# The causal mask ahead of the gates' exponentials: added by VectorE on the way out of PSUM, in place of an identity product on TensorE

## The chip, the cores and the metric

The kernel runs on one core of one Trainium2 chip. The metric is the device time of one execution in microseconds (us). Three runs of the kernel before gave 985.32, 985.60 and 986.42 us, a median of 985.6 us.

## The reference, cut to what matters

The reference is a two-layer encoder trunk on 256 positions of 1024 numbers. Each layer has three sub-layers: a SwiGLU block, a mixer and another SwiGLU block. The mixer has two head groups side by side, a differential attention and an mLSTM. The change is in the mLSTM, in the matrix of weights that a position `j` gives to an earlier position `s`:

```
causal = jnp.tril(jnp.ones((CHUNK, CHUNK), dtype=bool))
D = jnp.where(causal, b[..., :, None] - b[..., None, :] + log_i[..., None, :], -jnp.inf)
m_inter = b + m_prev[..., None]
m = jnp.maximum(m_inter, D.max(-1))
w = jnp.exp(D - m[..., None]) * jnp.einsum('bhcjd,bhcsd->bhcjs', q, k)
```

`exp(D - m)` is wanted, with zero where `s` is later than `j`. The kernel computes the exponent as a product of gate rows, adds a mask that is 0 where `s <= j` and -1e30 elsewhere, and takes the exponential. It works in chunks of 128 positions, of which there are two.

## The kernel before, in words

**Tiling.** The 256 positions are two tiles, `t` = 0 and 1, of 128 rows. A weight arrives in pieces of 128x2048 fp32 numbers, by a DMA that SyncE (SP) issues (L272). Each half of a piece is split in two: ScalarE (ACT) rounds it to a high part `wh` (L278), and VectorE (DVE) subtracts that from the raw half to get the low part `wl` (L279). The activations are split in the same way into `th` and `tl`. Every large product is then three matmuls of 512 columns, high by high, high by low and low by high (`mm3`, L393 to L395), so TensorE (PE) runs thousands of them, and DVE and ACT feed it with split weights.

**The mixer.** `traverse` (L699) walks through 84 steps of three matmuls each. They make six groups of 512 columns: the mLSTM's q and k (ahead of the walk and in its first steps), the attention's q, its k, the mLSTM's v, the attention's v, and the output gate. A group's two tiles end in two PSUM banks, named `pin`, which are read out as soon as they are complete. For the attention's q and k that reading is `rope` (L979): ACT scales the bank into `rv` (L984), DVE multiplies it by the cosines into `ra` (L985) and, in two halves, by the sines into `rb` (L988), and adds the two (L989). `roped` (L992) then transposes the finished `ra` on PE in four blocks (L805), and ACT copies them out as `qkT` (L996).

**What stands between the steps.** The table `AT` gives the step at which each of 32 side stages is written: the gates, the convolution, the rotary transposes, the scores. Both calls of `gate_exps` and the first call of `roped` stand at step 24. `conv` for the q blocks stands at 31, `gate_decays` at 36, `conv_silu` at 38, and `weighted_qk` and the `roped` call for the first tile of k both at 40.

**Order on an engine.** Each engine executes its instructions in the order of its own list. That list is made when the kernel is built: a scheduler takes the program as written, its priorities (`high_priority` around the reading of banks) and its own estimates of durations, and puts the instructions in order. An instruction waits until the ones that it depends on are done, and everything behind it on the same engine waits too.

**The code that the change touches.** `constants_mix` (L178) loads the mask by DMA into a temporary `mraw` (L200), and ACT copies the mask and the 128x128 identity into fp32r tiles, `c_mask` (L203) and `c_identr` (L204). `gate_exps` (L919) runs for each of the two tiles and in each of the two layers, four times in all. It starts a PSUM bank `pe` with a product of the gate rows `ul` and `md` (L924), adds the mask to the bank with a product of the identity and the mask, repeated for the four heads (L925), and ACT takes the exponential of the bank into `eE` (L927, recorded under L256, the line of the helper `func`). `eE` is read in `intra_weights` (L976).

**The stages around it.** `gate_decays` (L930) makes the decays `ex` on DVE (L935 to L937), ACT takes their exponential, and `eh` is their low part (L942). `conv` (L828) is a causal convolution of four blocks, on ACT for its first tap (L834) and on DVE for the other three (L837). `weighted_qk` (L944) starts with two small PE products of `eh` (L949), three small transposes (L952) and two transposes of k (L958). In PE's list these are followed by the four transposes of the `ra` of k's first tile (L805).

Of the kernel before, what the change touches and what calls it, by code (L numbers as in the profile page):

```python
# [15 lines left out]
F32 = mybir.dt.float32  # L16
F32R = mybir.dt.float32r
AF = mybir.ActivationFunctionType
ALU = mybir.AluOpType
# [3 lines left out]
P = 128  # L23
# [28 lines left out]
def _lam_init(l):  # L52
    return 0.8 - 0.6 * math.exp(-0.3 * l)
# [74 lines left out]
class _Trunk:  # L128
# [49 lines left out]
    def constants_mix(self):  # L178
        nc, a = self.nc, self.a
        c1 = self.const.tile([P, sum(math.prod(v) for _, v in C1)], F32, name="c_1")  # L180
        self.after(nc.sync.dma_start(c1, a["c1"]), [self.load])
        at = 0
        for name, shape in C1:
            n = math.prod(shape)
            dims = " ".join("abc"[:len(shape)])
            v = c1[:, at:at + n].rearrange(f"p ({dims}) -> p {dims}", **dict(zip("abc", shape)))
            setattr(self, name, v)
            at += n
        self.scan = self.const.tile([100, 2, S], F32, name="c_scan")
        self.after(nc.sync.dma_start(self.scan.rearrange("p a b -> p (a b)"), a["scan"]), [self.load])  # L190
        for l in range(L):
            nc.gpsimd.tensor_scalar(self.gda[:, l:l + 1], self.gda[:, l:l + 1], 1.0 - _lam_init(l), None, op0=ALU.mult)
        nc.gpsimd.tensor_scalar(self.gml, self.gml, 0.5, None, op0=ALU.mult)
        self.wgc = self.const.tile([P, L, KT, 16], F32R, name="c_wgc")
        ia = nc.scalar.activation(self.wgc[:, :, :, 0:8], self.wg, AF.Copy)
        iv = nc.vector.tensor_tensor(self.wgc[:, :, :, 8:16], self.wg, self.wgc[:, :, :, 0:8].bitcast(F32), op=ALU.subtract)
        self.fold = self.const.tile([16, 8], F32, name="c_fold")
        self.after(nc.vector.tensor_tensor(self.fold, self.ident[0:16, 0:8], self.ident[0:16, 8:16], op=ALU.add), [iv])
        mraw = self.t2("mraw", (P, P))
        self.after(nc.sync.dma_start(mraw, a["mask"]), [self.load])  # L200
        self.mask = self.const.tile([P, P], F32R, name="c_mask")
        self.identr = self.const.tile([P, P], F32R, name="c_identr")
        nc.scalar.activation(self.mask, mraw, AF.Copy)  # L203
        self.after(nc.scalar.activation(self.identr, self.ident, AF.Copy), [ia])  # L204

        lamv = self.t2("lamv", (P, L, 4, 64))
        self.after(nc.sync.dma_start(lamv.rearrange("p l a b -> p l (a b)"), a["lam"].partition_broadcast(P)), [self.load])
        prod = self.t2("lamp", (P, L, 2, 64))
        nc.vector.tensor_tensor(prod, lamv[:, :, 0::2, :], lamv[:, :, 1::2, :], op=ALU.mult)
        sums = self.const.tile([P, L, 2], F32, name="c_lams")  # L210
        nc.vector.tensor_reduce(sums, prod, axis=AX.X, op=ALU.add)
        self.lamsum = sums
        self.neglam = self.const.tile([P, L], F32, name="c_neglam")

        self.g2 = self.ded.tile([P, NT, 2, 4, 32], F32, name="g2")
        nc.gpsimd.memset(self.g2, 0.0)
        self.hot = self.const.tile([100, 4], F32, name="c_hot")
        ih = nc.vector.tensor_reduce(self.hot, self.ident[0:100].rearrange("p (a b) -> p b a", a=4)[:, 0:4, :], axis=AX.X,
                                     op=ALU.add)
        self.after(ih, [iv])  # L220
        self.ul = self.ded.tile([100, S], F32R, name="ul")
        nc.gpsimd.memset(self.ul.bitcast(F32), 0.0)
        for p in (64, 96):
            nc.gpsimd.memset(self.ul[p:p + 4].bitcast(F32), 1.0)
        self.md = self.ded.tile([100, NT, 4, P], F32R, name="md")
        nc.gpsimd.memset(self.md.bitcast(F32), 0.0)
        for t in range(NT):
            i = nc.scalar.activation(self.md[0:36, t], self.hot[0:36].unsqueeze(2).broadcast_to([36, 4, P]), AF.Copy)
            self.after(i, [ia])
        self.hotp = self.const.tile([36, 2, P], F32R, name="c_hotp")  # L230
        self.after(nc.vector.tensor_copy(self.hotp.rearrange("p a (b d) -> p (a b) d", b=2),
                                         self.hot[0:36].unsqueeze(2).broadcast_to([36, 4, 64])), [iv])
        self.qk = self.ded.tile([P, 4, S], F32, name="qk")
        self.qd = self.ded.tile([P, 2, CH], F32, name="qd")
        self.vx = self.ded.tile([P, NT, 4, P + 1], F32, name="vx")
        self.wt = self.ded.tile([P, NT, 2, 2, P], F32, name="wt")
        nc.gpsimd.memset(self.vx, 1.0)
        self.xpad = self.ded.tile([P, 4, S + 3], F32, name="xpad")
        nc.gpsimd.memset(self.xpad[:, :, 0:3], 0.0)
# [444 lines left out]
class _Mixer:  # L684
# [234 lines left out]
    def gate_exps(self, t):  # L919

        tr = self.tr
        cols = slice(t * P, t * P + P)
        pe = tr.bank_bk()
        self.mm(pe, tr.ul[:, cols], tr.md[:, t].rearrange("p h j -> p (h j)"), start=True, stop=False)  # L924
        self.mm(pe, tr.identr, tr.mask.unsqueeze(1).broadcast_to([P, 4, P]), start=False, stop=True)  # L925
        eE = tr.t2("eE")
        tr.func(eE, pe, AF.Exp)  # L927
        self.eE.append(eE)

    def gate_decays(self):  # L930
# [251 lines left out]
```

## Time and profile before

| | kernel before |
|---|---|
| median of three runs | 985.6 us |
| the profiled execution's own time | 986.18 us |
| its span | 984.4 us |
| PE busy | 976.0 us (99%) in 4629 matmuls |
| DVE busy | 606.4 us (62%) in 863 instructions |
| ACT busy | 528.4 us (54%) in 869 instructions |
| GpSimd (POOL) busy | 27.6 us (3%) |
| HBM read | 177.01 MB |
| mean granted PE clock | 0.998 of full speed |

The span runs from the first recorded instruction of the program to its last. The execution's own time is 1.78 us longer, for what lies around the span. "Busy" counts the time in which an engine has an instruction in flight. Matmuls overlap one another, so PE's busy time is not a count of its work: when one matmul takes over from another, the next one's start tells more than its duration. In a list of instructions in order of time, the columns are start and duration in us, engine, line, operation, the tile written and the tiles read, the shape, and how many instructions are merged in the row. What stands in brackets is the engine's idle time ahead of it and what ended it.

### The profile page before, as it was taken

What the parts mean: (1) busy time and instruction counts of PE and PEld (TensorE: products, weight loads), DVE (VectorE), ACT (ScalarE), POOL (GpSimd) and SP (SyncE); (2) the same over time, 40 slices, a digit from 0 to 9 for tenths busy, and PEclk for the clock granted to TensorE, in tenths of its full rate; (3) what the DMA queues carried; (4) which work ended last, traced back from release to release, by engine and by line L of the source; (5) the groups of instructions that cost most, each with busy time, mean ns of one, the idle gap of its engine ahead of it and who ended that gap; (6) DMA issues with size and microseconds to landing.
All of it is one profiled execution on the core that took longest, in us unless ns stands there. A gap on an engine that the chain in (4) does not pass through costs nothing.

```text
span 984.4 us, 12032 instructions
## 1 busy us (share of the span) xinstructions
PE 976.0 (99%) x4629; PEld 800.2 (81%) x4629; DVE 606.4 (62%) x863; ACT 528.4 (54%) x869; POOL 27.6 (3%) x51
## 2 busy tenths in 40 slices
PE   9999999999999999999999999999999999999997
PEld 6888888888788888888888888888888888888885
DVE  6755554589867655555485645455888586554542
ACT  7744444477856545444375544444778475544431
POOL 1000000000010000000000000000001000000000
PEclk9999999999999999999999999999999999999999
DMA  8954545336352844464356455443454257544511
GB/s 304 346 217 174 197 169 192 124 129 216 123 196 95 312 167 179 184 239 171 129 207 242 162 188 207 178 163 119 166 207 167 90 205 263 195 171 171 210 48 43
DMA packets 27640, 178.84 MB, mean 182 GB/s; under 512 B 3034, under 2 KB 4186, under 8 KB 6846
## 3 DMA queue, kind: packets, MB, share of 16 engines
q1 hardware_dynamic: 27006, 177.46, 48.9%
q8 instruction: 36, 0.59, 0.2%
q10 hardware_dynamic: 576, 0.61, 0.2%
q14 instruction: 22, 0.18, 0.0%
HBM read 177.01 MB, written 1.05 MB: 181 GB/s over the span
## 4 chain that ended last, share of the span: by engine, by line
PE 99%; DMA 1%; DVE 0%; SPq 0%; ACT 0%; POOLq 0%; issue 0%; DVEq 0%; ACTq 0%
PE pin L393 21%; PE pin L395 20%; PE pin L394 20%; PE bk L393 10%; PE bk L395 10%; PE bk L394 10%; PE ptr L523 2%; PE ptr L805 1%; PE ptr L412 1%; PE bk L1017 1%; PE bk L1057 1%; DMA x<-in_x_dram 1%; PE bk L372 0%; PE bk L370 0%; PE bk L1097 0%; PE bk L371 0%
## 5 line engine op out<-in xcount | busy, mean ns | idle before, releaser
L279 DVE TENSOR_TENSOR wl<-wr,wh 128x1024 fp32r<-128x1024 f32 x324 | 389.4, 1223 | 223.4 <-ACT wh L278 213.7
L278 ACT ACTIVATE wh<-wr 128x1024 fp32r<-128x1024 f32 x324 | 336.5, 1057 | 190.4 <-PE pin L395 102.1
L393 PE MATMUL pin<-wh,th 128*128 128x512 f32 x880 | 349.5, 398 | 0.0
L395 PE MATMUL pin<-wh,tl 128*128 128x512 f32 x880 | 343.4, 391 | 0.0
L394 PE MATMUL pin<-wl,th 128*128 128x512 f32 x880 | 343.3, 390 | 0.0
L395 PEld LDWEIGHTS pin<-wh,tl 128*128 128x128 f32 x880 | 165.2, 188 | 35.2
L393 PEld LDWEIGHTS pin<-wh,th 128*128 128x128 f32 x880 | 165.4, 188 | 33.3 <-ACT vd L1002 0.8
L394 PEld LDWEIGHTS pin<-wl,th 128*128 128x128 f32 x880 | 165.5, 188 | 32.3
L393 PE MATMUL bk<-wh,hh 128*128 128x512 f32 x352 | 140.0, 398 | 0.0
L395 PE MATMUL bk<-wh,hl 128*128 128x512 f32 x352 | 137.6, 393 | 0.0
L394 PE MATMUL bk<-wl,hh 128*128 128x512 f32 x352 | 137.6, 391 | 0.0
L526 ACT ACTIVATE hh<-ptr 128x256 fp32r<-128x256 f32 x88 | 33.2, 377 | 93.3 <-PE ptr L523 75.6
L256 ACT ACTIVATE sil<-pin,rs 128x256 f32<-128x256 f32 x86 | 40.5, 472 | 73.7 <-PE pin L395 69.8
L395 PEld LDWEIGHTS bk<-wh,hl 128*128 128x128 f32 x352 | 66.1, 188 | 13.8
L394 PEld LDWEIGHTS bk<-wl,hh 128*128 128x128 f32 x352 | 66.2, 188 | 12.8
L393 PEld LDWEIGHTS bk<-wh,hh 128*128 128x128 f32 x352 | 66.1, 188 | 12.8
L527 DVE TENSOR_TENSOR hl<-ptr,hh 128x256 fp32r<-128x256 f32 x88 | 37.1, 422 | 54.3 <-ACT hh L526 51.5
L516 DVE SCALAR_TENSOR_TENSOR h<-pin,rs,sil 128x256 f32<-128x256 f32 x86 | 41.2, 480 | 30.2 <-ACT sil L256 30.2
L401 POOL TENSOR_TENSOR rs<-s,c_half 128x1 f32<-128x1 f32 x24 | 13.1, 553 | 774.2 <-DVE s L438 774.2
L523 PEld LDWEIGHTS ptr<-c,h 128*128 128x128 f32 x176 | 24.7, 140 | 11.5
L523 PE MATMUL ptr<-c,h 128*128 128x128 f32 x176 | 33.4, 271 | 0.0
L454 ACT ACTIVATE junk<-bk 128x512 bf16<-128x512 f32 x24 | 14.2, 592 | 31.1 <-PE bk L395 31.1
(179 smaller groups left out, 586.8 us busy)
## 6 DMA issues: line engine op xcount, KB each, us to landing
wr<-in_w_dram SPq DMA_DIRECT2D x162, 1024.0 KB, 4.9
gpost<-in_gpost_dram SPq DMA_DIRECT2D x6, 512.0 KB, 6.2
wr<-in_w_dram SPq DMA_DIRECT2D x2, 512.0 KB, 7.1
wr<-in_w_dram SPq DMA_DIRECT2D x3, 256.0 KB, 5.2
x<-in_x_dram SPq DMA_DIRECT2D x3, 256.0 KB, 5.8
out_dram<-x SPq DMA_DIRECT2D x2, 256.0 KB, 2.1
x<-in_x_dram SPq DMA_DIRECT2D x2, 128.0 KB, 2.7
wr<-in_w_dram ACTq DMA_DIRECT2D x1, 256.0 KB, 3.5
```

The costliest lines, as they stand in the source:

```text
L256: i = self.nc.scalar.activation(*args, **kw)
L278: ia = nc.scalar.activation(hi, raw[:, j], AF.Copy)
L279: iv = nc.vector.tensor_tensor(lo, raw[:, j], hi.bitcast(F32), op=ALU.subtract)
L393: mm(ps, xh, wh, start=start, stop=False)
L394: mm(ps, xh, wl, start=False, stop=False)
L395: mm(ps, xl, wh, start=False, stop=stop)
L401: self.nc.gpsimd.tensor_tensor(r, ss, self.half[:, :width], op=ALU.pow)
L454: return nc.scalar.activation(self.junk_tile(), po[hf], AF.Square, scale=1.0 / (16 if half else 32), accum_out=ss[:, hf:hf + 1])
L516: nc.vector.scalar_tensor_tensor(h, pin[:, 256:512], r, sil, op0=ALU.mult, op1=ALU.mult)
L523: nc.tensor.transpose(ptr[:, k, :], h[:, k * P:(k + 1) * P], self.ident)
L526: nc.scalar.activation(hh, ptr, AF.Copy)
L527: nc.vector.tensor_tensor(hl, ptr, hh.bitcast(F32), op=ALU.subtract)
```

## The change

The mask is no longer accumulated in PSUM. The product of the gate rows is now a group of its own, VectorE adds the mask to the bank while it writes the sum to the SBUF tile `eE`, and ACT takes the exponential in place. The mask is loaded straight into its fp32 tile, and the two copies on ACT and the fp32r identity are gone.

```diff
-        mraw = self.t2("mraw", (P, P))
-        self.after(nc.sync.dma_start(mraw, a["mask"]), [self.load])
-        self.mask = self.const.tile([P, P], F32R, name="c_mask")
-        self.identr = self.const.tile([P, P], F32R, name="c_identr")
-        nc.scalar.activation(self.mask, mraw, AF.Copy)
-        self.after(nc.scalar.activation(self.identr, self.ident, AF.Copy), [ia])
+        self.mask = self.const.tile([P, P], F32, name="c_mask")
+        self.after(nc.sync.dma_start(self.mask, a["mask"]), [self.load])
...
-        self.mm(pe, tr.ul[:, cols], tr.md[:, t].rearrange("p h j -> p (h j)"), start=True, stop=False)
-        self.mm(pe, tr.identr, tr.mask.unsqueeze(1).broadcast_to([P, 4, P]), start=False, stop=True)
+        self.mm(pe, tr.ul[:, cols], tr.md[:, t].rearrange("p h j -> p (h j)"), start=True, stop=True)
         eE = tr.t2("eE")
-        tr.func(eE, pe, AF.Exp)
+        self.tt(eE.rearrange("p (h j) -> p h j", h=4), pe.rearrange("p (h j) -> p h j", h=4),
+                tr.mask.unsqueeze(1).broadcast_to([P, 4, P]), op=ALU.add)
+        tr.func(eE, eE, AF.Exp)
```

Four lines fewer stand ahead of the rest of the file in the changed kernel, and from `gate_exps` on its lines are lower by three or four: L989 of before is L986 there, L805 is L801.

The change also makes the scheduler put other things in another order. Three places show it, all in the first layer; the second layer reads the same, with other numbers in the names. A number behind a tile's name tells which buffer it is. The first place is PE, at the products of the gates. Before:

```order
L805 MATMUL ptr_234_2010<-c_0_95,nat_222_1917 128x128 x4
L924 MATMUL bk_236_2025<-md_603,ul_599 128x512
L925 MATMUL bk_236_2025<-c_mask_584,c_identr_585 128x512
L924 MATMUL bk_238_2030<-md_603,ul_599 128x512
L925 MATMUL bk_238_2030<-c_mask_584,c_identr_585 128x512
L805 MATMUL ptr_241_2036<-c_0_95,ra_224_1932 128x128 x4
```

And in the changed kernel:

```order
L801 MATMUL ptr_233_2006<-c_0_95,nat_221_1913 128x128 x4
L920 MATMUL bk_235_2021<-md_599,ul_595 128x512
L920 MATMUL bk_237_2026<-md_599,ul_595 128x512
L801 MATMUL ptr_240_2032<-c_0_95,ra_223_1928 128x128 x4
L389 MATMUL pin_241_2038<-wh_37_0_1957,th_203_1792 128x512
```

The two mask products are gone, and nothing else in PE's list has moved, here or anywhere. The second place is DVE, just behind that point, at the first split half of piece 40. Before (`ra_228` is the rotated second tile of the attention's q, `ex` the decays):

```order
L279 TENSOR_TENSOR wl_40_0_2184<-wr_40_2182,wh_40_0_2185 128x1024
L989 TENSOR_TENSOR ra_228_1975<-ra_228_1975,rb_229_1976 128x512
L935 TENSOR_TENSOR ex_250_2129<-gt_231_1989 36x128
L936 TENSOR_TENSOR ex_250_2129<-mp_232_1995,gt_231_1989 36x128
L937 SCALAR_TENSOR_TENSOR ex_250_2129<-gt_231_1989 36x256
```

And in the changed kernel (`ra_227` is the same tile there):

```order
L275 TENSOR_TENSOR wl_40_0_2180<-wr_40_2178,wh_40_0_2181 128x1024
L922 TENSOR_TENSOR eE_236_2023<-bk_235_2021,c_mask_582 128x512
L922 TENSOR_TENSOR eE_238_2028<-bk_237_2026,c_mask_582 128x512
L986 TENSOR_TENSOR ra_227_1971<-ra_227_1971,rb_228_1972 128x512
L932 TENSOR_TENSOR ex_249_2125<-gt_230_1985 36x128
L933 TENSOR_TENSOR ex_249_2125<-mp_231_1991,gt_230_1985 36x128
L934 SCALAR_TENSOR_TENSOR ex_249_2125<-gt_230_1985 36x256
```

The two adds of the mask have come in between; the rest keeps its order. The third place is DVE again, from the second half of piece 40 on. Before, eight convolution steps stand just ahead of it. `ra_244` and `rb_245` are the first tile of the attention's k, `ra_248` and `rb_249` its second:

```order
L279 TENSOR_TENSOR wl_40_1_2194<-wr_40_2182,wh_40_1_2195 128x1024
L837 SCALAR_TENSOR_TENSOR conv_235_2016<-xpad_614,c_1_570,conv_235_2016 128x256 x4
L279 TENSOR_TENSOR wl_41_0_2219<-wr_41_2217,wh_41_0_2220 128x1024
L942 TENSOR_TENSOR eh_251_2135<-ex_250_2129,eh_251_2135 4x128
L985 TENSOR_TENSOR ra_244_2086<-rv_243_2085,c_1_570 128x512
L988 TENSOR_TENSOR rb_245_2087<-rv_243_2085,c_1_570 128x8x32 x2
L279 TENSOR_TENSOR wl_41_1_2231<-wr_41_2217,wh_41_1_2232 128x1024
L989 TENSOR_TENSOR ra_244_2086<-ra_244_2086,rb_245_2087 128x512
```

In the changed kernel, four convolution steps stand just ahead of it, and k's two tiles are `ra_243` with `rb_244`, and `ra_247` with `rb_248`:

```order
L275 TENSOR_TENSOR wl_40_1_2190<-wr_40_2178,wh_40_1_2191 128x1024
L833 SCALAR_TENSOR_TENSOR conv_234_2012<-xpad_610,c_1_570,conv_234_2012 128x256 x4
L275 TENSOR_TENSOR wl_41_0_2215<-wr_41_2213,wh_41_0_2216 128x1024
L833 SCALAR_TENSOR_TENSOR conv_234_2012<-xpad_610,c_1_570,conv_234_2012 128x256 x4
L982 TENSOR_TENSOR ra_243_2082<-rv_242_2081,c_1_570 128x512
L985 TENSOR_TENSOR rb_244_2083<-rv_242_2081,c_1_570 128x8x32 x2
L939 TENSOR_TENSOR eh_250_2131<-ex_249_2125,eh_250_2131 4x128
L275 TENSOR_TENSOR wl_41_1_2227<-wr_41_2213,wh_41_1_2228 128x1024
L982 TENSOR_TENSOR ra_247_2118<-rv_246_2117,c_1_570 128x512
L275 TENSOR_TENSOR wl_42_0_2301<-wr_42_2299,wh_42_0_2302 128x1024
L985 TENSOR_TENSOR rb_248_2119<-rv_246_2117,c_1_570 128x8x32 x2
L986 TENSOR_TENSOR ra_243_2082<-ra_243_2082,rb_244_2083 128x512
```

The sum that finishes k's first tile, the last row of both pieces, now has the cosine and sine products of k's second tile and one more weight half (`wl_42_0`) ahead of it; before, these stand behind it. `eh` has moved behind the products of k's first tile.

On ACT the two exponentials of `eE` move from either side of the four `conv` instructions to behind the next copy of `qkT` and the next weight half, the silu of q and k (`qk`) moves behind one more bank's reading and one more weight half, and the two copies at the start are gone. On SP the mask's DMA is issued three weight pieces earlier. POOL's list is the same.

## The prediction

> **What bounds the kernel now.** I read the page first, its busy times and the chain that ended last:
>
> ```profile
> PE 976.0 (99%) x4629; PEld 800.2 (81%) x4629; DVE 606.4 (62%) x863; ACT 528.4 (54%) x869; POOL 27.6 (3%) x51
> PE 99%; DMA 1%; DVE 0%; SPq 0%; ACT 0%; POOLq 0%; issue 0%; DVEq 0%; ACTq 0%
> ```
>
> PE is in flight for 99% of the span, and the chain is PE from end to end. A change is therefore worth what it does to PE: products that PE no longer issues, and time in which PE has to stand still. The 62% of DVE is an average, and says nothing of the place where the change puts its work. So I read the list of instructions in order of time around that place, PE first:
>
> ```profile
> 224.38 0.47 PE L924 MATMUL bk<-md,ul 100*128 100x512 f32 x1
> 224.70 0.40 PE L925 MATMUL bk<-c_mask,c_identr 128*128 128x512 f32 x1
> 224.93 0.39 PE L924 MATMUL bk<-md,ul 100*128 100x512 f32 x1
> 225.16 0.39 PE L925 MATMUL bk<-c_mask,c_identr 128*128 128x512 f32 x1
> 225.40 0.27 PE L805 MATMUL ptr<-c,ra 128*128 128x128 f32 x1
> ...
> 237.36 0.44 PE L949 MATMUL bk<-eh,c_hotp 36*128 36x128 f32 x2
> 237.72 0.34 PE L952 MATMUL bk<-c,ex 4*128 4x4 f32 x3
> 238.00 0.44 PE L958 MATMUL bk<-c,qk 128*128 128x128 f32 x2
> 238.39 0.30 PE L805 MATMUL ptr<-c,ra 128*128 128x128 f32 x1
> ```
>
> The upper five rows are the products that the change halves; the lower four are the place some 13 us later where PE first needs something that DVE makes behind the new adds. Then DVE over the same stretch:
>
> ```profile
> 225.21 1.22 DVE L279 TENSOR_TENSOR wl<-wr,wh 128x1024 fp32r<-128x1024 f32 x1
> 226.35 0.69 DVE L989 TENSOR_TENSOR ra<-ra,rb 128x512 f32<-128x512 f32 x1
> 226.95 0.28 DVE L935 TENSOR_TENSOR ex<-gt 36x128 f32<-36x128 f32 x1
> 227.15 0.28 DVE L936 TENSOR_TENSOR ex<-mp,gt 36x128 f32<-36x128 f32 x1
> 227.35 0.41 DVE L937 SCALAR_TENSOR_TENSOR ex<-gt 36x256 f32<-36x256 f32 x1
> 227.69 3.25 DVE L837 SCALAR_TENSOR_TENSOR conv<-xpad,c,conv 128x256 f32<-128x256 f32 x8
> 230.86 1.21 DVE L279 TENSOR_TENSOR wl<-wr,wh 128x1024 fp32r<-128x1024 f32 x1
> 232.00 1.66 DVE L837 SCALAR_TENSOR_TENSOR conv<-xpad,c,conv 128x256 f32<-128x256 f32 x4
> 233.58 1.21 DVE L279 TENSOR_TENSOR wl<-wr,wh 128x1024 fp32r<-128x1024 f32 x1
> 234.83 0.28 DVE L942 TENSOR_TENSOR eh<-ex,eh 4x128 fp32r<-4x128 f32 x1
> 235.14 0.69 DVE L985 TENSOR_TENSOR ra<-rv,c 128x512 f32<-128x512 f32 x1
> 235.75 0.76 DVE L988 TENSOR_TENSOR rb<-rv,c 128x256 f32<-128x256 f32 x2
> 236.42 1.22 DVE L279 TENSOR_TENSOR wl<-wr,wh 128x1024 fp32r<-128x1024 f32 x1
> 237.56 0.69 DVE L989 TENSOR_TENSOR ra<-ra,rb 128x512 f32<-128x512 f32 x1
> ```
>
> Here DVE has no idle time worth the name. Its last row ends at 237.56 + 0.69 = 238.25, and PE's transposes of that very `ra`, the first tile of k, start at 238.39, 0.14 later. So PE takes the result as soon as it is there: at this point DVE is already as late as it can be without holding PE up. The second layer reads the same:
>
> ```profile
> 723.03 0.68 DVE L989 TENSOR_TENSOR ra<-ra,rb 128x512 f32<-128x512 f32 x1
> ...
> 723.86 0.63 PE L805 MATMUL ptr<-c,ra 128*128 128x128 f32 x4
> ```
>
> 723.03 + 0.68 = 723.71, and 0.15 later PE starts. Work that DVE gets ahead of this sum is paid by PE in full.
>
> **The change part by part.**
>
> *The mask products go.* A matmul's duration (0.40) is not its price, since the next one starts while it is in flight. By starts, the first mask product takes 224.93 - 224.70 = 0.23 us and the second 225.40 - 225.16 = 0.24, or 0.47 a layer and 0.94 in all.
>
> *The adds come.* Each reads a 128x512 bank and a mask repeated for four heads. The nearest row is the pre-norm's multiplication of a 128x512 bank with a broadcast gain:
>
> ```profile
> 201.99 1.29 DVE L417 TENSOR_TENSOR xg<-ptr,c 128x512 f32<-128x512 f32 x2 [0.43 <-PE ptr L412]
> ```
>
> Two in a row end after 1.29, and the next instruction starts just under 0.1 before an end (a split half lasts 1.22 and is followed after 1.14), so two adds push the rest back by 1.2. They need both banks: the second product now starts at 224.70 and is done near 225.1, before DVE is through with the half that it began at 225.21, so there is no wait. From below they cannot cost less than the same shape among SBUF tiles (226.95 - 226.35 = 0.60 each, so again 1.2); from above I take a pass over twice the columns, 1.14 each, or 2.3.
>
> *Work moved ahead of k's first tile.* The lists in the section on the change show what now stands ahead of the sum that finishes it: besides the adds, the cosine product of k's second tile (235.75 - 235.14 = 0.61 by the same step of the first), its two sine products (236.42 - 235.75 = 0.67) and the split half `wl_42_0` (1.14). That is 2.42, more than the adds themselves.
>
> *The walk.* From 225.21 in the new order, by starts: half 1.14, two adds 1.20, the sum for q 0.60, the decays 0.74, four conv steps 1.58, half 1.14, four conv 1.58, half 1.14, four conv 1.58, cosine product 0.61, sine products 0.67, `eh` 0.28, half 1.14, cosine product 0.61, half 1.14, sine products 0.67, and the last sum to its end 0.69. That is 16.51 us, to 241.72 against 238.25 before: 3.47 later. By difference it is 1.20 + 2.42 = 3.62, less 0.14 for two short waits around `eh` that the new order has no more.
>
> *Does DVE wait for ACT in that walk?* ACT's rows in this stretch:
>
> ```profile
> 225.16 0.59 ACT L256 ACTIVATE eE<-bk 128x512 f32<-128x512 f32 x1
> 225.64 2.07 ACT L834 ACTIVATE conv<-xpad,c 128x256 f32<-128x256 f32 x4
> 228.09 0.59 ACT L996 ACTIVATE qkT<-ptr 128x512 f32<-128x512 f32 x1
> 228.56 1.06 ACT L278 ACTIVATE wh<-wr 128x1024 fp32r<-128x1024 f32 x1
> 229.51 0.63 ACT L256 ACTIVATE ex<-ex 36x512 f32<-36x512 f32 x1
> 230.16 1.28 ACT L250 ACT_TABLE_LOAD   x1
> 232.62 0.67 ACT L984 ACTIVATE rv<-pin,rs 128x512 f32<-128x512 f32 x1
> ```
>
> The last thing that DVE needs from ACT is the high part of `wl_42_0`. Ahead of its end stand, in the new order and by full durations: four conv 2.07, `qkT` 0.59, half 1.06, two exponentials 1.18, half 1.06, `ex` 0.63, table 1.28, `rv` 0.67, `eh` at most 0.63, half 1.06, `qkT` 0.59, `rv` 0.67, half 1.06: 12.55, so 237.7 counted from 225.16, and DVE comes to it at 239.2. It doesn't wait. The exponentials move to about 229, far ahead of their reader at step 61. The mask's earlier load and the two copies that ACT drops lie at 44 to 54 us, beside PE's work; I cost them at nothing, covered by that PE is never idle there.
>
> *What PE pays.* PE comes to `eh`'s products 0.47 earlier, at about 236.9, but `eh` is done 12.26 after 225.21, at 237.5. It waits some 0.6, does its seven small instructions by 238.7, and then stands until 241.72 + 0.14 = 241.86, where before it started at 238.39. Everything behind these transposes on PE's list, all later matmuls of the kernel, is 3.47 late, and the 0.47 saved is swallowed by the wait. Next late after them is nothing on DVE's side: the products behind read weights that DVE has split by then.
>
> *The sum.* 2 layers x 3.47 = +6.9 us. The profiled execution took 986.18 and would take 993.1; the median of the three runs is 0.58 below it, so the prediction is 985.6 + 6.9 = **992.5 us**, 0.7% slower. A measurement of this kernel can tell about 0.2%, or 2 us, from no change.
>
> **The rivals.**
>
> *The clock falls in the wait.* PE would stand still for 238.7 to 241.86, 3.2 us, a pause that the kernel has nowhere now. At the end of the program, after PE's last matmul, the granted clock fell:
>
> ```profile
> 977.67 0.39 PE L395 MATMUL bk<-wh,hl 128*128 128x512 f32 x1
> ...
> 978.00:981.00 3.00, 0.05 (x1) 0.00 (x0) 2.20 (x6) 0.69 (x2) 0.55 (x1) 1.00 0.00 0
> 981.00:984.40 3.40, 0.00 (x0) 0.00 (x0) 0.30 (x1) 0.00 (x0) 0.00 (x0) 0.55 0.44 154
> ```
>
> The column behind the five engines is PE's clock. A mean of 0.55 from 981.0 to 984.4 is full clock to 981.34 and half from there, 3.3 us after the last matmul's end at 978.06. The pause to come is 3.2 us, with little work in the 1.7 us before it. So it is close. The price is read at the program's start, where PE runs slow:
>
> ```profile
> 1.17 2.31 PE L382 MATMUL bk<-junk 128*128 128x512 bf16 x5 [1.17 <-DVE mp L906]
> ...
> 4.75 0.58 PE L382 MATMUL bk<-junk 128*128 128x512 bf16 x1
> ```
>
> From 1.17 to 4.75 + 0.58 = 5.33 the products last longer than the 0.39 that they take later: some 4 us at half speed, so about 2 us lost for each fall. With one fall the time is 994.5, with two 996.5. The Trainium skill states a rule for this ("TensorE: Matmul & The Clock Gate", Part 1): an idle window of about 3.4 us halves the array's clock, a busy window of the same length restores it, and the windows run freely, whatever the kernel does. By that page a fall would cost 1.7 us, an estimate from its window, and whether a pause that falls short of a window counts would hang on the phase. The trace agrees as far as it goes: 3.3 us to the fall at the end. No row shows what a pause of 3.2 us does. I give this 0.27.
>
> *Only the adds count.* If the moved steps cost PE nothing (because it needs k's second tile soon after anyway), DVE is 1.2 to 1.3 late a layer, and the time is 988.1. Against it stands that DVE takes its list in order, and the transposes of the first tile come 14 us ahead of those of the second. 0.05.
>
> *DVE has room after all, and the products saved are what is left.* This is the case that is not slower: 985.6 - 0.94 = 984.7, no change that can be told. Its place is the same pair of rows. It decides if `ra` is done by 238.25 - 0.47 = 237.78 in the changed kernel, so if the walk takes 12.6 us instead of 16.5; DVE would have to do in it what it takes 3.9 us less for than any row allows. For it speaks only that PE's record has a step of 0.14 between the end of `ra` and its own start, which could be something else than a wait. 0.05. That the change doesn't do what it says I leave out: the lists show the products gone and the adds there.
>
> **How the numbers follow.** The forecast has 0.63, the falling clock 0.27, the two others 0.05 each. The low end of the range is the sum with 0.7 a layer less, 985.6 + 2 x 2.77 = 991.1, rounded to 991.0: 0.6 a layer is what I may have wrong in 17 steps read to 0.03 or so each, and 0.1 what later waits on DVE could give back. The high end holds the dear adds (1.1 more a layer, 994.7), one fall of the clock (994.5) and most of two: 996.0. Left out are the two cheap rivals and the worst of two falls, under 0.2. Slower by over 0.2% is everything but the last rival: 0.95. Within 0.2% is 0.04 of it, and 0.01 stays for faster, for which I see no mechanism.
>
> **What would show it.** Right: PE has four matmuls fewer and DVE four instructions more; the list of who waited for whom, in which this stretch does not appear now, gets two waits of PE's transposes (L801) for DVE's sum (L986) of some 3 us each, and two shorter ones of L946 for `eh` (L939); from 225 to 242 us DVE is full, and PE has its hole just ahead of 241.9 and, in the second layer, of about 730.8; the chain gets some 3% of DVE. The mean clock tells of the rival: a half-clock stretch behind a hole. Wrong: the adds at well over 0.7 us each; `ra` done before 241; PE at its transposes without a wait; or a later place that gives the delay back, so that the last layer's matmuls are less than 6 us late.

## The result, and the profile after

In five runs the changed kernel took 997.4 us in the median (995.73 to 998.61), against 985.46 us (985.12 to 986.42) in five runs of the kernel before on the same chip: a ratio of 1.0119, with a 95% interval of 1.0108 to 1.0130. That is 11.9 us slower, 4.9 us above the 992.5 that was forecast and 1.4 us above the end of its range. The profiled execution took 997.4 us with a span of 995.6, 11.2 us longer than the span before.

The page of the changed kernel, first its busy times and, from the second part, the granted clock in 40 slices, then the chain that ended last:

```profile
PE 979.8 (98%) x4625; PEld 803.0 (81%) x4625; DVE 608.8 (61%) x867; ACT 528.2 (53%) x867; POOL 27.8 (3%) x51
PEclk9999999998999999999999999999989999999999
PE 94%; DVE 4%; issue 1%; DMA 1%; ACT 0%; SPq 0%; POOLq 0%; DVEq 0%; ACTq 0%
```

PE has its four matmuls fewer and DVE its four instructions more. DVE now holds 4% of the chain that was PE from end to end. And the clock has two slices with an 8, one in each layer, that were not there. The first two rows of the list of who waited for whom, for PE:

```profile
PE ptr L801 <- DVE ra L986: 6.5, 2, 3.3
PE bk L946 <- DVE eh L939: 1.3, 2, 0.7
```

Columns are the total in us, the times and the longest. These are the four waits that the prediction named: two of some 3 us for the sum of k's first tile, two short ones for `eh`. DVE in the first layer, from the split half ahead of the adds to the sum:

```profile
225.12 1.22 DVE L275 TENSOR_TENSOR wl<-wr,wh 128x1024 fp32r<-128x1024 f32 x1
226.25 1.28 DVE L922 TENSOR_TENSOR eE<-bk,c_mask 128x512 f32<-128x512 f32 x2
227.45 0.68 DVE L986 TENSOR_TENSOR ra<-ra,rb 128x512 f32<-128x512 f32 x1
...
238.65 0.68 DVE L982 TENSOR_TENSOR ra<-rv,c 128x512 f32<-128x512 f32 x1
239.25 1.22 DVE L275 TENSOR_TENSOR wl<-wr,wh 128x1024 fp32r<-128x1024 f32 x1
240.38 0.75 DVE L985 TENSOR_TENSOR rb<-rv,c 128x256 f32<-128x256 f32 x2
241.06 0.68 DVE L986 TENSOR_TENSOR ra<-ra,rb 128x512 f32<-128x512 f32 x1
```

The adds take 227.45 - 226.25 = 1.20 us, the three moved rows 241.06 - 238.65 = 2.41, and the walk from 225.12 to 241.74 takes 16.62, where 16.51 was worked out. PE at the same place:

```profile
237.53 0.43 PE L946 MATMUL bk<-eh,c_hotp 36*128 36x128 f32 x2 [0.65 <-DVE eh L939]
237.89 0.34 PE L949 MATMUL bk<-c,ex 4*128 4x4 f32 x3
238.17 0.44 PE L955 MATMUL bk<-c,qk 128*128 128x128 f32 x2
241.88 1.09 PE L801 MATMUL ptr<-c,ra 128*128 128x128 f32 x4 [3.27 <-DVE ra L986]
...
243.20 0.63 PE L390 MATMUL pin<-wl,th 128*128 128x512 f32 x1
243.62 0.63 PE L391 MATMUL pin<-wh,tl 128*128 128x512 f32 x1
...
245.76 0.52 PE L390 MATMUL pin<-wl,th 128*128 128x512 f32 x1
246.12 0.40 PE L391 MATMUL pin<-wh,tl 128*128 128x512 f32 x1
246.35 0.39 PE L389 MATMUL pin<-wh,th 128*128 128x512 f32 x1
```

The transposes start at 241.88, 0.02 from the forecast, which is closer than the working deserves: the walk is 0.11 longer than forecast and begins 0.09 earlier in this execution (225.12 in place of 225.21). But the products behind them last 0.63 and start 0.42 apart, until about 246.0; from there they last 0.39 and start 0.23 apart, as everywhere else. The second layer shows the same stretch from 732.88 on.

When the clock changes is in the trace's record of it. In the changed kernel the clock is at half from 239.20 to 246.03 and from 730.72 to 737.55, 6.83 us each time. All changes in one trace lie a multiple of 3.413 us apart (in the kernel before, the rise at 5.15 and the fall at 981.37 are 286.0 of them apart). So I cut the trace on this grid. The windows view has stretch and length, busy time and instructions of PE, PEld, DVE, ACT and POOL, then the clock and two columns for DMA:

```profile
235.79:239.20 3.41, 2.17 (x12) 1.32 (x10) 3.35 (x7) 2.82 (x3) 0.00 (x0) 1.00 0.00 0
239.20:242.62 3.42, 0.74 (x4) 0.77 (x5) 3.42 (x8) 0.00 (x0) 0.00 (x0) 0.50 0.78 285
242.62:246.03 3.41, 3.41 (x10) 2.74 (x9) 0.46 (x2) 1.06 (x2) 0.00 (x0) 0.50 0.07 26
246.03:249.44 3.41, 3.41 (x16) 2.81 (x16) 2.34 (x2) 1.66 (x2) 0.00 (x0) 1.00 0.21 34
```

The fall comes at the end of a stretch in which PE was in flight for 2.17 of 3.41 us, with five large products and seven small ones. (A large product has 512 columns; the small ones are the two products of `eh` and five small transposes.) It is only 0.6 us after the last small one, and 2.7 us before PE starts again: most of the long wait was still to come. The rise comes here at the end of the first stretch that PE works through. With products 0.42 apart in place of 0.23, what is lost is about half of the time from the restart to the rise, (246.03 - 241.88)/2 = 2.07 us here, and (737.55 - 732.88)/2 = 2.33 in the second layer. With the 2 x 3.47 of the forecast that is 11.3 us, against 11.2 of the spans.

### The profile page after: what moved, and what is told of

Its sections match the earlier page's. It is cut to its first block, busy times and chain, and to the rows that moved or that the text cites. A ratio compares the mean times of both kernels' runs of the same rounds, so it can differ in the third digit from the quotient of the medians.

```text
span 995.6 us, 12029 instructions
## 1 busy us (share of the span) xinstructions
PE 979.8 (98%) x4625; PEld 803.0 (81%) x4625; DVE 608.8 (61%) x867; ACT 528.2 (53%) x867; POOL 27.8 (3%) x51
## 4 chain that ended last, share of the span: by engine, by line
PE 94%; DVE 4%; issue 1%; DMA 1%; ACT 0%; SPq 0%; POOLq 0%; DVEq 0%; ACTq 0%
PE pin L389 19%; PE pin L391 19%; PE pin L390 19%; PE bk L389 10%; PE bk L391 10%; PE bk L390 10%; PE ptr L519 2%; DVE wl L275 1%; DVE conv L833 1%; PE ptr L408 1%; PE ptr L801 1%; PE bk L1014 1%; DVE rb L985 1%; PE bk L1054 1%; DVE ra L982 1%
```

## The experiments

The theory after the result: the late sum costs what the prediction said, made of adds (1.2 a layer) and moved steps (2.4 a layer), and each hole also lowers the clock, because a stretch of the grid catches too little of PE's work. The rivals: the clock's record is no cost, and a further delay is missing; the clock falls only after a pause of some 3.3 us; the adds are all that costs; the order is all that costs. Each kernel was timed beside the kernel before on the same chip, in four groups, and a difference between two groups is taken between what each lost against its own kernel before. Its medians were 985.28 us (13 large products, the adds without the moved steps, the moved sum, GpSimd with the order held), 985.69 (30 small products, 6 large ones, GpSimd, adds at step 44), 985.33 (45 small products, the kernel before and the changed kernel with the order held) and 985.18 (adds at step 44, again).

**Filling the hole with large products.**

```diff
         ptk = tr.bank_bk((P, 2, P))
         for pr in range(2):
-            self.T(ptk[:, pr, :], self.kT[:, pr, 0:P], tr.ident)
+            last = self.T(ptk[:, pr, :], self.kT[:, pr, 0:P], tr.ident)
+        bank = tr.bank_bk()
+        xh = self.xT[0][0][0]
+        for _ in range(13):
+            i = self.mm(bank, xh[:, 0, :], xh.rearrange("p k c -> p (k c)"), start=True, stop=True)
+            tr.after(i, [last])
+            last = i
...
```

Lines left out here make the four transposes of k's first tile wait for the last of them as well.

> The changed kernel, with 13 extra 512-column products on PE (3.0 us at 0.23 each, by the starts of the products before), written to a bank that nobody reads, between the transposes of k's convolution and the waiting transposes of the first k tile, in both layers. PE has work in the hole, but starts behind it when it did before. Theory (late sum plus clock): the delay of 3.47 us a layer stays, the clock stays full, and the time is 985.5 + 7 = 992.5 us. Rival (the slow clock is only recorded and costs nothing, so some further delay is missing from the sum): 997, as the changed kernel. Rival (the wait is no wait for the sum but PE's own pace): 997.4 + 2 x 3.0 = 1003.

Measured: 992.66 us (992.45 to 993.19), a ratio of 1.0075 (1.0063 to 1.0088). PE in the first layer:

```profile
237.64 3.20 PE L961 MATMUL bk<-th 128*128 128x512 f32 x13
241.17 0.63 PE L801 MATMUL ptr<-c,ra 128*128 128x128 f32 x4 [0.33 <-DVE ra L995]
241.55 0.48 PE L389 MATMUL pin<-wh,th 128*128 128x512 f32 x1
241.87 0.40 PE L390 MATMUL pin<-wl,th 128*128 128x512 f32 x1
```

PE does more work and the kernel is 4.6 us faster than the changed one (7.38 us slower than before, in place of 11.94). The transposes still wait for the sum, so the 13 products do not delay them, but the products behind them last 0.48 and then 0.40, and the clock's record has no half-speed stretch in either layer. The delay without the clock is 7.4 us, with an interval of 6.2 to 8.7 (6.9 was forecast), and the clock's share of the loss is about 4.6, against the 2.07 + 2.33 worked out above. Both rivals of this expectation fall.

**Filling it with small products.** The same edit with small transposes in place of the large products, first 30 and then 45 of them:

```diff
+        bank = tr.bank_bk((P, 64, 4))
+        for n in range(45):
+            i = self.T(bank[:, n, :], self.ex[0:4, 0, 0:P], tr.ident[0:4, 0:4])
+            tr.after(i, [last])
+            last = i
```

> The changed kernel with 30 extra transposes of a 4x4 block in the hole instead of the 13 large products, all into a bank that nobody reads: at 0.09 us each, by the starts of the three such transposes before, PE has an instruction in flight for 2.8 us of the hole, but hardly any columns stream. If the clock goes by whether PE has something in flight, it stays full, and the time is 992.5 us, as with the large products. If it goes by how much PE streams in one span of the 3.41-us grid, it falls as in the changed kernel, and the time is 997 us (996 to 998.5).

> The changed kernel with 45 of the 4x4 transposes in each hole instead of 30, since 30 lasted only 2.1 us (0.07 each) and left a wait of 1.3. 45 take 3.15 us, so that PE has an instruction in flight nearly without a break, as with the 13 large products. If having something in flight keeps the clock up: 992.6 us, as with those. If the clock goes by what PE streams: 996 to 998.5, as the changed kernel.

Measured: 996.62 us (995.6 to 999.24), a ratio of 1.0118 (1.0105 to 1.0132), with 30, and 997.19 (995.18 to 998.44), 1.0115 (1.0100 to 1.0131), with 45. So nothing is gained over the changed kernel. PE with 45 of them, and then the windows on the grid:

```profile
239.64 2.94 PE L960 MATMUL bk<-c,ex 4*128 4x4 f32 x45
242.99 1.09 PE L801 MATMUL ptr<-c,ra 128*128 128x128 f32 x4 [0.42 <-DVE ra L994]
243.73 0.78 PE L389 MATMUL pin<-wh,th 128*128 128x512 f32 x1
244.30 0.63 PE L390 MATMUL pin<-wl,th 128*128 128x512 f32 x1
```

```profile
239.42:242.84 3.42, 3.15 (x47) 2.90 (x46) 3.42 (x7) 0.30 (x1) 0.00 (x0) 1.00 0.61 189
242.84:246.25 3.41, 3.26 (x10) 2.81 (x11) 1.35 (x5) 0.60 (x1) 0.00 (x0) 0.50 0.30 123
```

PE was in flight for 3.15 of 3.42 us, and still the clock fell. The busy column is therefore not what decides. That it goes by how much PE streams fits, since a 4x4 transpose streams next to nothing; but these fillers differ from the 13 products in being transposes, too, and which of the two counts no run here separates. The runs' spread fits the clock: of the four runs with 45, 998.44 and 997.96 have a mean clock of 0.992, 996.42 has 0.994 and 995.18 has 0.995. Not all of it comes from the holes: the profiled one, 998.44, has one more half-speed stretch at the program's start, from 7.32 to 10.73.

**Filling half of it.** The first edit with 6 large products in place of 13.

> The changed kernel with 6 instead of 13 of the large extra products in each hole: 1.4 us of it is filled, and a pause of about 1.9 us is left, as long as that of the kernel with the moved sum and no adds. Theory: 992.5 us and what the clock takes; the half-speed stretch now comes only where the grid lies so that one span of it catches the whole pause, and lasts one span where PE works through it, so 0 to 1.7 us for each layer: 993.5 to 996. Rival (a pause under 3 us never costs clock): 992.5.

Measured: 994.61 us (994.5 to 994.81), a ratio of 1.0094 (1.0080 to 1.0108). PE's waits for the sum, and then its windows on the grid, two stretches of the first layer and two of the second:

```profile
PE ptr L801 <- DVE ra L995: 3.8, 2, 1.9
```

```profile
236.85:240.26 3.41, 2.47 (x13) 1.77 (x13) 3.35 (x6) 1.60 (x2) 0.00 (x0) 1.00 0.19 36
240.26:243.67 3.41, 1.93 (x11) 1.70 (x12) 2.68 (x8) 0.60 (x1) 0.00 (x0) 1.00 0.68 276
...
728.37:731.78 3.41, 1.52 (x10) 1.03 (x9) 3.41 (x8) 0.32 (x1) 0.00 (x0) 1.00 0.87 308
731.78:735.19 3.41, 3.41 (x10) 2.64 (x9) 0.70 (x2) 1.33 (x2) 0.00 (x0) 0.50 0.01 2
```

Both layers have the same wait of 1.89 us. In the first the grid cuts it in two, each part has six or seven large products beside it, and the clock holds. In the second one stretch catches all of it, and the clock falls for one stretch, which PE works through: some 3.41/2 = 1.7 us. Measured, it is 1.5 us more than with 13 products (8.9 against 7.4, each beside its own kernel before). So a pause of 1.9 us can cost clock, and in these two layers the place of the grid decided it.

**The adds without the moved steps.** The changed kernel, with two instructions of DVE held behind the sum of k's first tile:

```diff
+            if (i % PIECES_LAYER, j) in ((42, 0),):
+                self.after(iv, [self.first])
...
-            tt(a8, v8, tr.rope[:, 0, t, :].unsqueeze(1).broadcast_to([P, 8, 64]), op=ALU.mult)
+            i = tt(a8, v8, tr.rope[:, 0, t, :].unsqueeze(1).broadcast_to([P, 8, 64]), op=ALU.mult)
+            if len(self.rot) == 3:
+                tr.after(i, [tr.first])
...
-            tt(a, a, b, op=ALU.add)
+            i = tt(a, a, b, op=ALU.add)
+            if len(self.rot) == 2:
+                tr.first = i
```

> The changed kernel with its two adds a layer, but on DVE the first product of k's second tile and the split half wl_42_0 are held behind the sum of k's first tile, as they stand before. The adds are paid, the moved work is not. Theory: PE waits about 1 us a layer for the sum, 1.20 less 0.1 each, so 985.5 + 2.2 = 987.7 us if the clock stays full; if a pause of 1 us together with the wait of 0.7 for eh is enough to make the clock fall, 2 to 2.5 us more for each fall, so 990 to 992.5. Rival (the adds themselves or their reading of PSUM are what is dear, and the order is worth nothing): 997, as the changed kernel.

Measured: 990.91 us (988.75 to 991.55), a ratio of 1.0053 (1.0041 to 1.0066). PE at the transposes, and the windows on the grid around them:

```profile
238.70 0.63 PE L803 MATMUL ptr<-c,ra 128*128 128x128 f32 x4 [0.88 <-DVE ra L990]
```

```profile
236.05:239.46 3.41, 1.88 (x14) 1.50 (x14) 3.35 (x7) 1.86 (x3) 0.00 (x0) 1.00 0.27 43
239.46:242.87 3.41, 3.41 (x10) 2.64 (x9) 2.92 (x8) 1.56 (x2) 0.00 (x0) 0.50 0.65 269
```

The wait is 0.88 in place of 3.27, so the moved steps were worth 2.39 us of it, 2.42 by the prediction. What is left is the adds' 2.2 us and the clock: two waits of 0.65 and 0.88, neither of them a pause of even 1 us, with seven small products in between, fell into one stretch and cost a whole one at half speed, in both layers: 2.2 + 2 x 1.7 = 5.6, and 990.91 - 985.28 = 5.6 was measured. The clock costs more here than the wait does.

**A moved sum without adds.** The kernel before, with the sum held back:

```diff
-                tt(b8[:, :, lo:lo + 32], v8[:, :, hi:hi + 32], sn, op=ALU.mult)
-            tt(a, a, b, op=ALU.add)
+                i = tt(b8[:, :, lo:lo + 32], v8[:, :, hi:hi + 32], sn, op=ALU.mult)
+            if len(self.rot) == 3:
+                tr.after(tr.first, [i])
+            i = tt(a, a, b, op=ALU.add)
+            if len(self.rot) == 2:
+                tr.first = i
```

> The kernel before with its mask products and without adds, but on DVE the sum of k's first tile is held behind the cosine and sine products of k's second tile (1.28 us), and the scheduler puts the split half there too. The moved work is paid, the adds are not. Theory: PE waits some 2 us a layer, so 985.5 + 3.8 = 989.3 us with the clock full, and 2 to 2.5 us more for each fall of the clock, so up to 994. Rival (order is worth nothing): 985.5, as before. Whether the clock falls here tells how long a pause it takes: by a rule that a pause must be about 3.3 us it does not fall.

Measured: 991.57 us (990.79 to 993.62), a ratio of 1.0065 (1.0051 to 1.0078). The split half did not move there after all; `qd` and `wem` did, with a wait of 0.29. The wait of PE is 1.99 us in both layers. PE's transposes, and then the windows on the grid, first layer and second:

```profile
240.48 0.63 PE L805 MATMUL ptr<-c,ra 128*128 128x128 f32 x4 [1.99 <-DVE ra L991]
...
727.98 1.09 PE L805 MATMUL ptr<-c,ra 128*128 128x128 f32 x4 [1.99 <-DVE ra L991]
```

```profile
235.75:239.16 3.41, 2.74 (x15) 1.86 (x13) 3.12 (x8) 2.89 (x3) 0.00 (x0) 1.00 0.28 82
239.16:242.58 3.42, 2.10 (x12) 1.82 (x13) 3.24 (x6) 0.65 (x2) 0.00 (x0) 1.00 0.73 292
...
723.86:727.27 3.41, 2.14 (x12) 1.34 (x11) 3.13 (x8) 2.29 (x3) 0.00 (x0) 1.00 0.32 74
727.27:730.68 3.41, 2.70 (x9) 2.34 (x10) 2.63 (x4) 0.60 (x1) 0.00 (x0) 0.50 0.56 238
```

The same hole, twice, in one execution: the grid cuts it at 239.16 in the first layer, 1.3 us before PE starts again, and at 727.27 in the second, 0.7 us before. In the first layer the clock held, in the second it fell, so a pause of some 3.3 us is not needed. And PE was in flight for 2.10 us where it held and for 2.14 where it fell; the first has eight large products in it (and so has the stretch ahead of it), the second five and seven small ones. Two waits and one fall make 2 x 1.99 + (730.68 - 727.98)/2 = 5.3 us; the profiled execution is 5.4 us above that of the kernel before, and the median 6.3, with an interval of 5.0 to 7.7. There is no add in this kernel, so a late sum costs this whatever makes it late.

**Neither adds nor products.** GpSimd zeroes the exponentials above the diagonal; the mask in the exponent is left out:

```diff
-        self.tt(eE.rearrange("p (h j) -> p h j", h=4), pe.rearrange("p (h j) -> p h j", h=4),
-                tr.mask.unsqueeze(1).broadcast_to([P, 4, P]), op=ALU.add)
-        tr.func(eE, eE, AF.Exp)
+        tr.func(eE, pe, AF.Exp)
+        e4 = eE.rearrange("p (h j) -> p h j", h=4)
+        tr.nc.gpsimd.affine_select(e4, e4, [[0, 4], [1, P]], ALU.is_ge, 0.0, base=0, channel_multiplier=-1)
```

> No mask in the exponent: GpSimd zeroes the exponentials above the diagonal behind ScalarE; neither mask products nor adds are there, and nothing holds the order, which the scheduler makes anew. It puts the same steps of k's second tile ahead of the sum of the first as in the changed kernel, although there is no add. If the order is the larger part of the delay: two waits of PE of some 2.3 us, +4.6 us with the clock full, and 1.4 to 3.4 for the clock: 991.5 to 993.5 us. If the adds were what costs: 985, or 984.5 with the products saved.

Measured: 995.81 us (994.2 to 996.82), a ratio of 1.0105 (1.0091 to 1.0118), above what was expected. DVE in the first layer:

```profile
233.91 0.86 DVE L830 SCALAR_TENSOR_TENSOR conv<-xpad,c,conv 128x256 f32<-128x256 f32 x1
234.81 0.60 DVE L936 TENSOR_TENSOR eh<-ex,eh 4x128 fp32r<-4x128 f32 x1
...
237.86 0.68 DVE L979 TENSOR_TENSOR ra<-rv,c 128x512 f32<-128x512 f32 x1
238.46 1.22 DVE L272 TENSOR_TENSOR wl<-wr,wh 128x1024 fp32r<-128x1024 f32 x1
239.60 0.75 DVE L982 TENSOR_TENSOR rb<-rv,c 128x256 f32<-128x256 f32 x2
240.27 0.68 DVE L983 TENSOR_TENSOR ra<-ra,rb 128x512 f32<-128x512 f32 x1
```

The sum has the same three steps ahead of it as in the changed kernel, with no add in the program. So the adds are not needed for the scheduler to turn them round; what does it here was not taken apart. The two upper rows are one part of why it came out later than expected: a step of the convolution took 0.86 and `eh` 0.60, where such steps take 0.47 and 0.28 in the kernels without GpSimd's selects. Both lie at the end of GpSimd's two selects (225.43 to 235.28); other DVE rows during them are not longer, and what lengthens these two was not taken apart. With them the sum ends 16.14 us after the split half that starts at 224.81, against 13.04 before (225.21 to 238.25), so it is 3.1 us late in place of 2.3. The other and larger part is the clock: the two half-speed stretches cost 2.4 and 2.7 in the profiled execution, the slowest of the four, where 1.4 to 3.4 was expected for both together.

**The order put right.** The last edits hold three instructions behind the sum: the second half of piece 41 and the first of 42 (`in ((41, 1), (42, 0))` in place of `in ((42, 0),)` in the diff of the adds without the moved steps) and the first product of k's second tile. One does that to the changed kernel as it is, one to the kernel before, one to the GpSimd kernel, and one also moves the adds:

```diff
-AT = (0, 2, 6, 6, 7, 22, 24, 24, 24, 24, 36, 31, ...
+AT = (0, 2, 6, 6, 7, 22, 24, 24, 44, 44, 36, 31, ...
```

> The changed kernel with the adds where the change puts them (step 24), and the second split half of piece 41, the first of piece 42 and the first product of k's second tile held behind the sum of k's first tile. The adds push the sum back by 1.2 us and the split half that is held back gives 1.14 of it back, so PE waits only for eh, 0.65 us a layer, against 0.47 of products saved: +0.7 us, 986.2. If the clock falls with that wait (0.65 us and seven small products in one span of the grid): up to 1.7 us more for a layer, up to 989.6.

> The kernel before with the same three instructions of DVE held behind the sum of k's first tile as in the kernel that moves the adds to step 44, and the mask still a product. The sum comes 1.14 us earlier, but PE does not wait for it there before either, beyond the 0.14 that any hand-over takes. If the gain of that kernel over before comes from the mask products that it leaves out, this one is as before, 985.4 us. If it comes from the order, this one is as fast as that, 984.6.

> No mask in the exponent at all: GpSimd sets the exponentials above the diagonal to zero in SBUF behind ScalarE, so that neither the mask products nor the adds are there; and on DVE the second split half of piece 41, the first of piece 42 and the first product of k's second tile are held behind the sum of k's first tile. If the delay of that sum is all that the change costs, the sum comes earlier than before and the products saved are gained: 985.5 - 0.94 = 984.5 us. If GpSimd's work on SBUF slows DVE, or the products saved are hidden: 985.5 or more.

> The changed kernel (mask added by DVE) with both calls of the gates' exponentials moved from step 24 to step 44, behind the rotary transposes of k's first tile, and with the second split half of piece 41, the first of piece 42 and the first product of k's second tile held behind the sum of k's first tile. The adds then stand behind the sum, and nothing is moved ahead of it. If a late sum and the clock are all of the change's loss, PE has no wait there, and the time is 985.3 less the 0.94 of the mask products: 984.4 us; if the adds cost PE something wherever they stand (waits at the scores, for instance), 985.5 or more.

> The kernel with the adds at step 44 and nothing of k's second tile ahead of the sum of the first, once more, beside new runs of the kernel before. If the 0.94 us of mask products are gained, 0.9990 to 0.9991 of before; if the first measurement was the scatter of runs, 1.0.

| kernel | us, median | beside | ratio, 95% interval |
|---|---|---|---|
| adds at 24, order held | 985.72 | 985.33 | 1.0002 (0.9993 to 1.0011) |
| before, order held | 985.05 | 985.33 | 0.9998 (0.9989 to 1.0007) |
| GpSimd, order held | 985.12 | 985.28 | 0.9997 (0.9988 to 1.0006) |
| adds at 44, order held | 984.55 | 985.69 | 0.9991 (0.9982 to 1.0000) |
| the same, again | 984.51 | 985.18 | 0.9994 (0.9985 to 1.0003) |

With the adds where the change puts them and three instructions held, the 11.9 us are gone. PE's waits there:

```profile
PE bk L948 <- DVE eh L941: 1.3, 2, 0.7
PE bk L380 <- DVE mp L904: 1.2, 1, 1.2
```

The wait for the sum has gone, the one for `eh` is left, and the clock stays full (the second row is at the program's start). The expectation's +0.7 us doesn't follow from its own terms: 2 x (0.65 - 0.47) is 0.4, and 0.4 was measured, inside the scatter. With the adds at step 44 that wait goes too. What is left should be the 0.94 us of the mask products; both times the median was lower, by 1.1 and 0.7, but both intervals reach 1.0 or nearly, so a gain is likely and not shown. Neither did the order alone, on the kernel before, change anything that can be told, and with GpSimd 985.12 lies between the two cases expected. (The 0.14 "that any hand-over takes" is that of the sum; in the changed kernel PE starts on `eh` 0.06 us after it is done, at 237.53 after 237.47.)

## Why the prediction was wrong, step by step

- *What bounds the kernel, and where the change meets it.* Right. PE waits for the sum of k's first tile in both layers, and behind the program's start nowhere else for longer than for `eh`.
- *The products go, and their 0.47 a layer is swallowed by the wait for `eh`.* Right: 0.65 us of wait, about 0.6 forecast.
- *The adds cost 1.2 a layer.* Right: 1.20 by starts. The bound from above, 2.3, was not needed.
- *The moved steps cost 2.42 a layer.* Right: 2.41 by starts, and 2.39 came back when they were held behind the sum.
- *DVE does not wait for ACT in the walk.* Right: the rows of DVE there have no idle time ahead of them, and the walk took 16.62 against 16.51. The 0.11 is a small misreading: the forecast took off 0.14 for two short waits around `eh`, and they are still there (0.77 from the sine products to `eh` and 0.31 from `eh` to the next, where 0.67 and 0.28 were set down). So the sum is 16.62 - 13.04 = 3.58 late a layer, not 3.47.
- *The sum of +6.9 us.* Right for what it covers: with the clock kept up by filler, the delay was 7.4 us (6.2 to 8.7).
- *Only the adds count; DVE has room after all.* Both were rightly held unlikely: the moved steps were worth 2.39 us of the wait, and PE did stand for 3.27.
- *The clock falls in the wait: 0.27, some 2 us for a fall.* This is the step that failed: the forecast's sum has no term for the clock, which stands among the rivals, and two falls are left out of the range. The runs showed 4.4 to 4.6 us of it. The price of one fall was right, 2.07 and 2.33 in the profiled execution, with some luck in it: by where the grid lies, one fall cost from some 1.4 us (the moved sum) to 2.7 (GpSimd). The chance was not right. The clock fell in both layers of the profiled execution, and the lowest of the five runs, 995.73, is still 3 us above what filler gave. The high end of the range, built from one fall "and most of two", fell short by 1.4 us.

Why the chance was wrong: the row at the program's end showed a fall 3.3 us after the last matmul, and the prediction set that beside a pause of 3.2 us, as if 3.3 were the pause that it takes. But that row shows a stretch with almost no work in it, so it bounds the need from above only. In the kernel with the adds alone the clock falls with waits of 0.65 and 0.88. The Trainium skill's rule ("TensorE: Matmul & The Clock Gate", Part 1), that an idle window of about 3.4 us halves the clock, holds here as to the length of the window and its running freely: all changes are multiples of 3.413 us apart. Taken strictly, a pause of 3.2 us can't leave such a window idle. As to "idle" the runs differ from it: in the stretches before a fall that are shown above PE was in flight for 1.52 to 3.15 us.

What would have led to 997, with what the runs now show: PE stands for 0.6 and 3.2 us with only seven small products in between, some 5 us with little streaming, so that any grid of 3.41 us has a stretch with few large products in it: even where a border halves the 5 us, each side has 2.5 of them and 0.9 us of large products, four, and five did not hold the clock. Then two falls are the likeliest case, and 992.5 + 2 x 2 = 996.5, the number that the prediction had for them, with the 2.07 and 2.33 of the trace 996.9.

What stays open: the exact measure of "too little". In these traces the clock fell with five large products and seven small ones in a stretch, and held with six and seven small ones; where a mix of shapes lies is not known. Large products alone need not fill much of a stretch. The last matmuls of the kernel with the adds at step 44 show it, and the empty stretch behind them:

```profile
974.90:978.31 3.41, 1.54 (x7) 0.94 (x5) 1.62 (x4) 1.38 (x4) 0.55 (x1) 1.00 0.00 0
978.31:981.72 3.41, 0.00 (x0) 0.00 (x0) 1.38 (x3) 0.00 (x0) 0.00 (x0) 1.00 0.44 154
```

Seven large products, 1.54 us in flight, held the clock through the next stretch, where 3.15 us of small transposes did not. That the spread of the changed kernel's runs comes from where the grid lies is borne out by their mean clocks (0.992 for 997.40, 998.55 and 998.61, and 0.994 for 995.73 and 995.85), not tested by itself.

## What to carry to other kernels

Work put on an engine that is idle on average is priced at the place where its next reader stands, together with whatever the scheduler turns round there: here the adds cost 1.2 us a layer, the turned steps 2.4 and the clock some 2.3, and holding three instructions in place took all of it back. Where a change makes PE stand still, add what half speed costs behind the hole to the hole itself, even if it is under 1 us, when what lies around it is small products. (Two waits of 0.65 and 0.88 cost clock; with the order held, the one of 0.65 alone did not.) Read a fall of the clock on its grid, and count large products in each stretch of it; PE's busy time does not tell.

## What the hardware showed that was not expected

- The clock's changes lie on one grid of 3.413 us through a whole execution, and the same hole of 1.99 us cost clock in one layer and none in the other.
- Being in flight does not keep the clock up: 45 transposes of 4x4, 3.15 us in flight out of 3.42, did not, and 13 products of 512 columns did. 13 products that nobody needed, in each layer, made the changed kernel 4.6 us faster.
- A 4x4 transpose in a row of many starts every 0.06 us (45 in 2.94, with 0.2 for the last one's own duration), while three of them between other work took 0.28 from the first to what followed.
